# Weights of the experts fetched into the merged stream's memory, token tile by token tile

## The chip, the cores and the metric

The kernel runs on one core of a Trainium2 chip. The metric is device time in microseconds of one execution, as the median of the runs shown. A profile is taken of one more execution of the same program. TensorE is PE in the rows, VectorE DVE, ScalarE ACT, GpSimd POOL, SyncE SP.

## The reference, cut to what matters

Two transformer blocks for 512 tokens of width 1024, in float32. The change lies in the second block: the end of its token mixer and its mixture of experts.

```python
def token_mixer(...):                       # attention and state-space branch, then
    merged = g_attn * (attn @ nsa_w_o) + g_ssm * (ssm @ ssm_w_o)      # 512 x 1024
    return merged @ w_out                                            # 1024 x 1024

def hier_moe(h, ...):
    g_prob = softmax(xt @ w_group + b_group); g_p, g_idx = top_k(g_prob, 1)   # 4 groups
    e_logits = (xt @ w_expert + b_expert)[its group's 8]
    e_p, e_idx = top_k(softmax(e_logits), 2)                                 # 2 of 8
    w = g_p * e_p / sum(e_p)
    # each expert e on the rows routed to it, added up with weights w:
    (silu(xb @ w_gate[e]) * (xb @ w_up[e])) @ w_down[e]      # 32 experts, width 256
...
x = x + gate1 * token_mixer(norm1(x)); x = x + gate2 * hier_moe(norm2(x)); out = rmsnorm(x, final_g)
```

The last line is in short form: both norms are modulated by a vector c, and a final norm ends the program.

## The kernel before

The program is emitted by Python functions. A scheduler sets each engine's order of instructions from the order of emission and its own estimates of when operands are ready; every DMA that SyncE issues stands in SyncE's one row and waits there for its buffer.

**merge** (L1856) forms the merged stream in columns of 128 features by 512 tokens, transposed (features on partitions), and splits each into a rounded half `m_hi` (ACT, L1885) and a rest `m_lo` (VectorE, L1886), so that w_out's product is three products of halves. `m_hi` and `m_lo` hold all 512 tokens, 16 KB on each partition.

**Moe.mix_out** (L1940) is w_out's product with the residual. The first half of the output columns comes from `K.ts` (L252 to L254), over 4 groups of weights, in each over the 4 token tiles. The second half runs over token tiles t = 0 to 3 (L2057 to L2059), 24 products for each. After a tile, `residual` adds it to x (`xres` in the rows) and stores the new x into DRAM (`xa`, L1965). `logits0` and `logits1(t)` make the router's logits `lg` and the normed row h (L2014 on VectorE for the last tile), stored into DRAM as `hd` (L2039).

**Moe.route** (L2065) picks groups and experts on VectorE, ranks the tokens of each expert, and by products with one-hot matrices (`slots`, L2164: first `hb`, then `val`, then `vf`) makes the lists `idx`, `dst` and `wsl`. A gather on GpSimd (L2268) fetches the rows of `hd` for a pair of experts, two experts of 64 rows each. `spread` (L2308) transposes them. Its small tiles lie in the pool "eh".

**Moe.run** (L2366) goes through 17 entries: 16 pairs and, at position 12, one overflow entry whose expert number is read from `ove`. For each entry: `up` (L2322, 32 products: 8 slices k, gate and up, two experts), tanh and two products on ACT and VectorE, `down` (L2344), scatter into `yd`. Then the final norm reads `xa` and `yd`.

**The ring.** `load` (L2270) fetches the weights of an entry in units of 1 MB, one DMA at L2280 each: gate, up, down for both experts of a pair, 99 units in all. `raw` (L1931) gives the buffers in turn: 18 before, of 11 buffers of its own (pool "er"), 5 of pool "er2" in the memory of `m_hi` and `m_lo`, opened once these are closed, and the two halves of x. `fetch(n)` emits loads until n units are asked for: 11 in mix_out ahead of w_out's second half, 13 and 16 in `open` (the last three behind `self.stored`, the last store of hd), and 18 in `route`:

```python
hold = nc.sync.dma_start(K.dram.tile([128, 1], F32, name="hold"), self.xg[0][:, 0:1]).ins
with tc.issue_after(hold):
    self.fetch(sum(NR) + 2)
```

The hold (L2173) stores 4 bytes of each of the 128 rows of the first gathered tile into a DRAM tile that nobody reads. It waits for the gather, and the two units behind it wait for its issue.

Of the kernel before, what the change touches and what calls it, by code (L numbers as in the profile page):

```python
# [9 lines left out]
F32 = mybir.dt.float32  # L10
F32R = mybir.dt.float32r
# [7 lines left out]
T = 512  # L19
# [51 lines left out]
class Filler:  # L71


    def __init__(self):
        self.q = []
# [1777 lines left out]
                yield from K.ws_pieces(K.i["ssm_w_o_2"][0], c * 128, 256, shi, slo, 4, branch)  # L1853


def merge(K, st, gd, aT, m_hi, m_lo):  # L1856

    nc, tc, i = K.nc, K.tc, K.i
    P = lambda *a, **k: st.enter_context(K.pool(*a, **k))
    mp = P(name="mm_", bufs=1)  # L1860
    wp = P(name="mw", bufs=2)
    a_hi, a_lo = (mp.tile([128, 4, T], F32R, name=n) for n in ("a_hi", "a_lo"))
    for c in range(4):
        nc.scalar.copy(a_hi[:, c, :], aT[0][:, c, :])
        nc.vector.tensor_sub(a_lo[:, c, :], aT[0][:, c, :], a_hi[:, c, :].bitcast(F32))
    x = [(h[:, c, :], l[:, c, :]) for h, l in ((a_hi, a_lo), aT[1:]) for c in range(4)]
    for c in range(0, 8, 2):
        sg = {}
        for b in range(2):
            for e in range(2):  # L1870
                sg[b, e] = wp.tile([128, T], F32, name=f"sg{b}{e}")
                nc.sync.dma_start(sg[b, e], gd[b, c + e])
        aps = [K.mm() for _ in range(2)]
        for u in (4, 0):
            hi, lo = K.wload(i["nsa_w_o_2"][0][u * 128:(u + 4) * 128, c * 128:c * 128 + 256], 4, 256)
            for e in range(2):
                for k in range(4):
                    (xh, xl), s = x[u + k], slice(e * 128, e * 128 + 128)
                    nc.tensor.matmul(aps[e], hi[:, k, s], xh, start=u + k == 4, stop=False)
                    nc.tensor.matmul(aps[e], hi[:, k, s], xl, start=False, stop=False)  # L1880
                    nc.tensor.matmul(aps[e], lo[:, k, s], xh, start=False, stop=u + k == 3)
        for e, p in enumerate(aps):
            nc.vector.scalar_tensor_tensor(sg[0, e], sg[0, e], 1.0, p, op0=OP.add, op1=OP.mult)
            nc.gpsimd.tensor_add(sg[0, e], sg[0, e], sg[1, e])
            nc.scalar.activation(m_hi[:, c + e, :], sg[0, e], AF.Copy, scale=0.5)  # L1885
            nc.vector.scalar_tensor_tensor(m_lo[:, c + e, :], sg[0, e], 0.5, m_hi[:, c + e, :].bitcast(F32),  # L1886
                                           op0=OP.mult, op1=OP.subtract)


NE = 32  # L1890
# [1 line left out]
FAR = 128  # L1892
NPAIR = NE // 2
NOV = 15
NR = 11, 5
NX = 3
AHEAD = 2
FAR_AT = 12
# [6 lines left out]
class Moe:  # L1905
# [3 lines left out]
    def __init__(self, K, st):  # L1909

        nc, i = K.nc, K.i
        self.K, self.sc = K, []
        P = lambda *a, **k: st.enter_context(K.pool(*a, **k))
        cp = self.cp = P(name="ec", bufs=1, side="right")
        self.x = cp.tile([128, NT, D], F32, name="xres2")
        self.ss = cp.tile([128, 2, NT], F32, name="ss2")
        self.er = [P(name="er", bufs=NR[0], side="right")]
        self.nraw = 0
        flat = lambda a, k: a.rearrange("e (p k) n -> e p (k n)", k=k)
        self.wd = [flat(i[n][0], k) for n, k in (("moe_w_gate_2", 8), ("moe_w_up_2", 8), ("moe_w_down_2", 2))]  # L1920

        self.order = [8 * a + e for e in range(8) for a in range(2)]
        self.order.insert(FAR_AT, None)
        self.ready, self.loads = [], self.weights()
        self.cst = cp.tile([128, ECOLS], F32, name="ecst")
        nc.sync.dma_start(self.cst, i["ce"])
        self.xa = K.dram.tile([T, D], F32, name="xa")

        self.yd = K.dram.tile([2 * T, D], F32, name="yd")

    def raw(self):  # L1931

        k = self.nraw % (sum(NR) + 2)
        self.nraw += 1
        if k >= sum(NR):
            k -= sum(NR)
            return self.x[:, 2 * k:2 * k + 2, :].rearrange("p t n -> p (t n)")
        pool = next(p for j, p in enumerate(self.er) if k < sum(NR[:j + 1]))
        return pool.tile([128, 2048], F32, name="eraw")

    def mix_out(self, xd, mod, m_hi, m_lo):

        K, cp, x, ss = self.K, self.cp, self.x, self.ss
        nc, i = K.nc, K.i
        w = i["w_out_2"][0]
        for t in range(NT):
            nc.sync.dma_start(x[:, t, :], xd[t * 128:(t + 1) * 128, :])
        self.hd = K.dram.tile([T, D], F32, name="hd")
        self.lg = cp.tile([128, NT, 36], F32, name="lg")
        with K.pool(name="mo", bufs=2) as wp:  # L1950
# [56 lines left out]
            def logits1(t):  # L2007
# [28 lines left out]
                else:  # L2036
                    nc.scalar.activation(h, h, AF.Copy, scale=rs)
                    nc.gpsimd.tensor_add(h, h, sh2)
                self.stored = nc.sync.dma_start(self.hd[t * 128:(t + 1) * 128, :], h).ins  # L2039

            wt = []
            for u in range(4):
# [1 line left out]
                r3 = raw.rearrange("p (k n) -> p k n", k=2)  # L2044
                nc.sync.dma_start(r3, w[u * 256:(u + 1) * 256, 512:].rearrange("(k p) n -> p k n", p=128))
                wt.append(K.split(raw, pool=None if u < 3 else wp, bufs=3 if u < 3 else 1))
            self.fetch(NR[0])
            for t in range(NT):
                if t == 1:
                    logits0()  # L2050
                if t > 1:
                    logits1(t - 2)
                ps = K.mm()
                for k in range(8):
                    hi, lo = (a[:, (k % 2) * 512:(k % 2 + 1) * 512] for a in wt[k // 2])
                    tt = slice(t * 128, (t + 1) * 128)
                    nc.tensor.matmul(ps, m_hi[:, k, tt], hi, start=k == 0, stop=False)  # L2057
                    nc.tensor.matmul(ps, m_hi[:, k, tt], lo, start=False, stop=False)
                    nc.tensor.matmul(ps, m_lo[:, k, tt], hi, start=False, stop=k == 7)  # L2059
                residual(1, t, ps)  # L2060
            for t in (2, 3):
                logits1(t)

    def route(self):
# [15 lines left out]
        with K.pool(name="eh", bufs=2, side="right") as hp, ExitStack() as late:  # L2080
# [89 lines left out]
            q1 = places(rk, iota, "roh")  # L2170
            at = index(idx[:, :NPAIR], slots(q1, hb)[:, :NPAIR], T).ins
            self.gather(self.xg[0], idx[:, 0:1])
            hold = nc.sync.dma_start(K.dram.tile([128, 1], F32, name="hold"), self.xg[0][:, 0:1]).ins  # L2173
            with tc.issue_after(hold):
                self.fetch(sum(NR) + 2)
            late.enter_context(tc.issue_after(at))

            def softmax(src, m, n, nm):
# [134 lines left out]
    def up(self, xt, rw):  # L2313
# [2 lines left out]
        nc = K.nc  # L2316
        pg, pu = ph = [K.mm()[:, :256] for _ in range(2)]
        sl = EH if len(rw) == 2 else (slice(0, FAR),)
        for k in range(8):
            for n in range(2):  # L2320
                for s, r in zip(sl, rw):
                    nc.tensor.matmul(ph[n][s], xt[:, k, s], r[n][:, k * 256:(k + 1) * 256],  # L2322
                                     start=k == 0, stop=k == 7)
# [32 lines left out]
    def open(self, st, mod):  # L2356
# [1 line left out]
        self.g2 = bcast(K, st.enter_context(K.pool(name="ef", bufs=1)), mod["g2"], "g2row")  # L2358
        self.wp = st.enter_context(K.pool(name="ew", bufs=2))
        self.xg = [K.wraw() for _ in range(NX)]  # L2360

        self.fetch(NR[0] + 2)
        with K.tc.issue_after(self.stored):
            self.fetch(sum(NR))

    def run(self, st, out):  # L2366
        K = self.K
# [128 lines left out]
def block2(K, x, B, mats, mod, out):  # L2496
# [20 lines left out]
            nc.vector.tensor_sub(slo[:, c, :], sT[:, c, :], shi[:, c, :].bitcast(F32))  # L2517
        N.attend(aT, shi, slo, gd)
    mp = mst.enter_context(K.pool(name="mrg", bufs=1))
    m_hi = mp.tile([128, 8, T], F32R, name="m_hi")  # L2520
    m_lo = mp.tile([128, 8, T], F32R, name="m_lo")
    with ExitStack() as st:
        merge(K, st, gd, aT, m_hi, m_lo)
    alst.close()
    B.st.close()
    K.close_x()
    with ExitStack() as st:
        moe = Moe(K, st)
        moe.mix_out(xd, mod, m_hi, m_lo)
        mst.close()  # L2530
        moe.er.append(st.enter_context(K.pool(name="er2", bufs=NR[1])))
        moe.open(st, mod)
        moe.route()
        moe.run(st, out)


def body(tc, i, out):
# [66 lines left out]
```

## Time and profile before

| | us |
|---|---|
| runs | 1674.64, 1672.14, 1673.77; median 1673.77 |
| profiled execution, its own time | 1672.8 |
| its span, first to last instruction | 1671.0 |
| PE busy | 1564.5 (94%) |
| DVE busy | 933.6 (56%) |
| ACT busy | 635.6 (38%) |
| POOL busy | 235.7 (14%) |
| mean granted clock of PE | 0.981 |

The device time has 1.8 us around the span. Busy time is an average over stages with different limits; the page's slices of the span show the DMA engines at a tenth to seven tenths for most of it and at nine tenths or more in the last fifth, where the experts' weights are read.

### The profile page before, as it was taken

The numbers are of one execution on the slowest core, as the hardware profiler recorded it, in microseconds if no ns is written. First come the engines' busy times: TensorE is split into PE (matmuls) and PEld (weight loads), VectorE is DVE, ScalarE is ACT, GpSimd is POOL, SyncE is SP. The second block draws the span as 40 slices with busy tenths as digits, with TensorE's granted clock in tenths as the row PEclk, the third lists the DMA queues.
The fourth block names the chain that finished last, engine by engine and source line by source line (L and its number), as shares of the span: only waits on it lengthen the run. The fifth ranks groups of instructions, "written<-read, shape, count | busy, mean of one in ns | idle before, by whom it ended". The sixth has DMA issues, their size and how long they took to land. (4 is left out here: it accounts for less than half of the span.)

```text
span 1671.0 us, 25319 instructions
## 1 busy us (share of the span) xinstructions
PE 1564.5 (94%) x9568; PEld 1171.6 (70%) x9568; DVE 933.6 (56%) x2155; ACT 635.6 (38%) x1300; POOL 235.7 (14%) x270
## 2 busy tenths in 40 slices
PE   6999999999999999999999899999999988999981
PEld 5677777778777888788788667676678755554550
DVE  6764368558989866556576545555534463221114
ACT  4543346554422332345343555555643320010001
POOL 1212211100010000004220111121212221110102
PEclk9999999999999999999999999999999998999996
DMA  4221121137467967325863322111127869999994
GB/s 147 69 77 52 52 102 64 64 88 211 148 216 205 210 214 216 103 89 165 177 154 113 89 64 64 51 40 56 45 75 265 302 256 326 418 418 418 419 397 178
DMA packets 204305, 284.74 MB, mean 170 GB/s; under 512 B 75666, under 2 KB 150421, under 8 KB 191509
## 3 DMA queue, kind: packets, MB, share of 16 engines
q1 hardware_dynamic: 198370, 273.07, 49.6%
q0 software_dynamic: 4896, 8.40, 1.3%
q10 hardware_dynamic: 915, 1.64, 0.3%
q8 instruction: 76, 1.25, 0.3%
q14 instruction: 48, 0.39, 0.1%
HBM read 262.07 MB, written 30.43 MB: 175 GB/s over the span
## 5 line engine op out<-in xcount | busy, mean ns | idle before, releaser
L154 DVE TENSOR_TENSOR wlo<-wraw,whi 128x1024 fp32r<-128x1024 f32 x162 | 203.4, 1257 | 155.0 <-ACT whi L153 153.3
L153 ACT CAST whi<-wraw 128x1024 fp32r<-128x1024 f32 x164 | 171.6, 1049 | 243.3 <-PE mm L1055 71.9
L213 PE MATMUL mm<-hhi,whi 128*128 128x512 f32 x440 | 184.2, 419 | 5.4 <-DVE mx L1757 2.9
L215 PE MATMUL mm<-hhi,wlo 128*128 128x512 f32 x440 | 176.6, 402 | 0.1
L214 PE MATMUL mm<-hlo,whi 128*128 128x512 f32 x440 | 176.3, 401 | 0.0
L2322 PE MATMUL mm<-eraw,xt 128*64 128x256 f32 (+1 forms) x1024 | 126.8, 382 | 7.2 <-DMA eraw<-in_moe_w_up 3.6
L171 PE MATMUL mm<-hhi,whi 128*128 128x512 f32 x320 | 127.4, 398 | 0.2 <-ACT whi L153 0.2
L172 PE MATMUL mm<-hlo,whi 128*128 128x512 f32 x320 | 126.3, 395 | 0.0
L173 PE MATMUL mm<-hhi,wlo 128*128 128x512 f32 x320 | 125.9, 395 | 0.0
L2322 PEld LDWEIGHTS mm<-eraw,xt 128*64 128x64 f32 (+1 forms) x1024 | 84.2, 139 | 46.4 <-DMA eraw<-in_moe_w_up 5.6
L213 PEld LDWEIGHTS mm<-hhi,whi 128*128 128x128 f32 x440 | 83.0, 189 | 32.7 <-issue 8.3
L215 PEld LDWEIGHTS mm<-hhi,wlo 128*128 128x128 f32 x440 | 83.1, 189 | 20.5 <-issue 1.6
L214 PEld LDWEIGHTS mm<-hlo,whi 128*128 128x128 f32 x440 | 83.2, 189 | 18.7 <-issue 4.7
L1760 ACT ACTIVATE NP<-NP,mx 128x512 f32<-128x512 f32 (+3 forms) x128 | 72.1, 563 | 44.3 <-DVE mx L1757 43.6
L1757 DVE CUSTOM_DVE_ANT_0 NP<-mm,ncst 128x512 f32<-128x512 f32 (+3 forms) x128 | 61.4, 479 | 37.6 <-PE aux L1788 35.9
L171 PEld LDWEIGHTS mm<-hhi,whi 128*128 128x128 f32 x320 | 60.2, 188 | 15.4 <-issue 0.8
L1054 PE MATMUL mm<-wlo,ahi 128*128 128x512 f32 x176 | 69.3, 394 | 1.5 <-DVE wlo L154 1.5
L2348 DVE SCALAR_TENSOR_TENSOR ey<-mm,wsl,g2row 128x512 f32<-128x512 f32 x34 | 25.5, 750 | 80.4 <-PE mm L2344 80.4
L173 PEld LDWEIGHTS mm<-hhi,wlo 128*128 128x128 f32 x320 | 60.3, 188 | 14.3
L1053 PE MATMUL mm<-whi,ahi 128*128 128x512 f32 x176 | 69.9, 401 | 0.0
L172 PEld LDWEIGHTS mm<-hlo,whi 128*128 128x128 f32 x320 | 60.3, 188 | 13.6
L1055 PE MATMUL mm<-whi,alo 128*128 128x512 f32 x176 | 69.3, 394 | 0.0
(786 smaller groups left out, 3279.0 us busy)
## 6 DMA issues: line engine op xcount, KB each, us to landing
wraw<-in_w_in SPq DMA_DIRECT2D x68, 512.0 KB
eraw<-in_moe_w_gate SPq DMA_DIRECT2D x32, 1024.0 KB
eraw<-in_moe_w_up SPq DMA_DIRECT2D x32, 1024.0 KB
eraw<-in_moe_w_down SPq DMA_DIRECT2D x25, 1024.0 KB
araw<-in_ada_w SPq DMA_DIRECT2D x48, 512.0 KB
wraw<-in_w_gate SPq DMA_DIRECT2D x22, 512.0 KB
wraw<-in_w_up SPq DMA_DIRECT2D x22, 512.0 KB
wraw<-in_w_down SPq DMA_DIRECT2D x22, 512.0 KB
```

The lines of the kernel that those rows point to most:

```text
L153: nc.scalar.copy(hi[:, :m], raw[:, :m])
L154: (eng or nc.vector).tensor_sub(lo[:, :m], raw[:, :m], hi[:, :m].bitcast(F32))
L171: nc.tensor.matmul(o, hi[:, k, a:a + m], xhi[:, kk, :], start=kk == 0, stop=False)
L172: nc.tensor.matmul(o, hi[:, k, a:a + m], xlo[:, kk, :], start=False, stop=False)
L173: nc.tensor.matmul(o, lo[:, k, a:a + m], xhi[:, kk, :], start=False, stop=kk == nk - 1)
L213: nc.tensor.matmul(ps, hi, xhi[:, k, :], start=k == 0, stop=False)
L214: nc.tensor.matmul(ps, hi, xlo[:, k, :], start=False, stop=False)
L215: nc.tensor.matmul(ps, lo, xhi[:, k, :], start=False, stop=k == nk - 1)
L1053: nc.tensor.matmul(ps, a[:, tt], hi[:, k, :], start=kk == 0, stop=False)
L1054: nc.tensor.matmul(ps, a[:, tt], lo[:, k, :], start=False, stop=False)
L1760: nc.scalar.activation(p[:, :n], p[:, :n], AF.Exp, scale=-1.0, bias=m, accum_out=d)
L2322: nc.tensor.matmul(ph[n][s], xt[:, k, s], r[n][:, k * 256:(k + 1) * 256], start=k == 0, stop=k == 7)
```

## The change

The merged stream becomes four tiles `m`, one for each token tile, with both halves in each (128 x 2 x 8 x 128); `merge` writes each column in four pieces on ACT and on VectorE. A tile is free when the second half of w_out's product for its token tile is through, and the ring takes it then. The ring has 19 buffers: 11 of its own, tiles 0, 1, 2 of m, the first half of x, tile 3, one of pool "er2", the second half of x, and one of pool "er3", opened on the right side after `route` in memory of its pool "eh". `fetch` goes by tile: to 12, 13, 14 units behind tiles 0, 1, 2, to 15 ahead of tile 3, to 16 behind it, to 18 in `open`; the 19th is asked for in `run`. The hold is gone. In `up` the loop over gate and up stands outside the loop over k, so that all 16 gate products come ahead of the 16 up products.

```diff
-                nc.scalar.activation(m_hi[:, c + e, :], sg[0, e], AF.Copy, scale=0.5)
-            nc.vector.scalar_tensor_tensor(m_lo[:, c + e, :], sg[0, e], 0.5, m_hi[:, c + e, :].bitcast(F32),
-                                           op0=OP.mult, op1=OP.subtract)
+            for t in range(NT):
+                v = sg[0, e][:, t * 128:(t + 1) * 128]
+                hi, lo = (m[t][:, h, c + e, :] for h in range(2))
+                nc.scalar.activation(hi, v, AF.Copy, scale=0.5)
+                nc.vector.scalar_tensor_tensor(lo, v, 0.5, hi.bitcast(F32), op0=OP.mult, op1=OP.subtract)
...
     def raw(self):
-        k = self.nraw % (sum(NR) + 2)
+        k = self.nraw % (NER + 8)
         self.nraw += 1
-        if k >= sum(NR):
-            k -= sum(NR)
+        if k < NER:
+            return self.er[0].tile([128, 2048], F32, name="eraw")
+        k -= NER
+        if k in (3, 6):
+            k = k // 3 - 1
             return self.x[:, 2 * k:2 * k + 2, :].rearrange("p t n -> p (t n)")
-        pool = next(p for j, p in enumerate(self.er) if k < sum(NR[:j + 1]))
-        return pool.tile([128, 2048], F32, name="eraw")
+        if k in (5, 7):
+            return self.er[k // 2 - 1].tile([128, 2048], F32, name="eraw")
+        return self.mp.tile([128, 2048], F32, name="eraw", tag="m", bufs=NT)
...
-            self.fetch(NR[0])
+            self.fetch(NER)
             for t in range(NT):
                 if t == 1:
                     logits0()
                 if t > 1:
                     logits1(t - 2)
+                if t == 3:
+                    self.fetch(NER + 4)
...
                 residual(1, t, ps)
+                self.fetch(NER + (1, 2, 3, 5)[t])
...
             self.gather(self.xg[0], idx[:, 0:1])
-            hold = nc.sync.dma_start(K.dram.tile([128, 1], F32, name="hold"), self.xg[0][:, 0:1]).ins
-            with tc.issue_after(hold):
-                self.fetch(sum(NR) + 2)
...
-        for k in range(8):
-            for n in range(2):
+        for n in range(2):
+            for k in range(8):
                 for s, r in zip(sl, rw):
                     nc.tensor.matmul(ph[n][s], xt[:, k, s], r[n][:, k * 256:(k + 1) * 256],
                                      start=k == 0, stop=k == 7)
...
-        self.fetch(NR[0] + 2)
-        with K.tc.issue_after(self.stored):
-            self.fetch(sum(NR))
+        self.fetch(NER + 7)
...
-        mst.close()
-        moe.er.append(st.enter_context(K.pool(name="er2", bufs=NR[1])))
+        moe.er.append(st.enter_context(K.pool(name="er2", bufs=1)))
         moe.open(st, mod)
         moe.route()
+        moe.er.append(st.enter_context(K.pool(name="er3", bufs=1, side="right")))
         moe.run(st, out)
+    mst.close()
```

SyncE's row, before, from the first store of xa to the second turn of the ring (`xa` and `hd` are stores, `eraw<-in_moe...` units of weights, `xres_12812<-in_moe...` units into halves of x):

```order
267 L1965 DMA xa<-xres_12812 128x1024 x2
268 L2039 DMA hd<-wraw 128x1024
269 L1965 DMA xa<-xres_12812 128x1024
270 L2039 DMA hd<-wraw 128x1024
271 L1965 DMA xa<-xres_12812 128x1024
272 L2039 DMA hd<-wraw 128x1024
273 L2280 DMA eraw<-in_moe_w_down 128x2048
274 L2039 DMA hd<-wraw 128x1024
275 L2280 DMA eraw<-in_moe_w_gate 128x2048 x2
276 L2280 DMA eraw<-in_moe_w_up 128x2048 x2
277 L2173 DMA hold<-wraw 128x1
278 L2280 DMA xres_12812<-in_moe_w_down 128x2048 x2
279 L2280 DMA eraw<-in_moe_w_gate 128x2048 x2
```

SyncE's row after, the same place (the code's lines are moved by 20: L1985 is xa, L2059 hd, L2300 the units):

```order
267 L1985 DMA xa<-xres_12862 128x1024
268 L2300 DMA eraw<-in_moe_w_down 128x2048
269 L1985 DMA xa<-xres_12862 128x1024
270 L2300 DMA eraw<-in_moe_w_gate 128x2048
271 L2059 DMA hd<-wraw 128x1024
272 L1985 DMA xa<-xres_12862 128x1024
273 L2300 DMA eraw<-in_moe_w_gate 128x2048
274 L2059 DMA hd<-wraw 128x1024
275 L2300 DMA xres_12862<-in_moe_w_up 128x2048
276 L1985 DMA xa<-xres_12862 128x1024
277 L2300 DMA eraw<-in_moe_w_up 128x2048
278 L2059 DMA hd<-wraw 128x1024 x2
279 L2300 DMA eraw<-in_moe_w_down 128x2048
280 L2300 DMA xres_12862<-in_moe_w_down 128x2048
281 L2308 TENSOR_LOAD ove
```

Units 12 to 16 stand between the stores of the token tiles, the last two directly behind the last hd, and the hold and the wait behind it are gone; a load of `ove` stands ahead of the 19th unit.

VectorE's row, before, at the last logits of mix_out, the last steps of the reciprocal root and the first step of routing (`tgm`):

```order
1774 L262 TENSOR_SCALAR rsi<-msv 128x1
1775 L2014 TENSOR_TENSOR wraw<-xres_12812,G 128x1024
1776 L264 TENSOR_SCALAR rsy<-rsi 128x1
1777 L267 TENSOR_TENSOR rsa<-rsy 128x1
1778 L268 SCALAR_TENSOR_TENSOR rsb<-rsa,msv 128x1
```

```order
1783 L272 SCALAR_TENSOR_TENSOR rsy<-rsb,rsy 128x1
1784 L2021 SCALAR_TENSOR_TENSOR l_13004<-l_13004,rsy,rb 128x36
1785 L2026 SCALAR_TENSOR_TENSOR lg<-aux,rsy,l_13004 128x36
1786 L2094 TENSOR_REDUCE tgm<-lg 128x4
1787 L2095 TENSOR_TENSOR tge<-lg,tgm 128x16
```

VectorE's row after, the same place (L2034 is h = x G, L2046 the logits, L2117 routing's first step):

```order
1782 L272 SCALAR_TENSOR_TENSOR rsy<-rsb,rsy 128x1
1783 L2041 SCALAR_TENSOR_TENSOR l_13054<-l_13054,rsy,rb 128x36
1784 L2046 SCALAR_TENSOR_TENSOR lg<-aux,rsy,l_13054 128x36
1785 L2034 TENSOR_TENSOR wraw<-xres_12862,G 128x1024
1786 L2117 TENSOR_REDUCE tgm<-lg 128x4
1787 L2118 TENSOR_TENSOR tge<-lg,tgm 128x16
1788 L2121 SCALAR_TENSOR_TENSOR tge<-tge,ecst 128x16
```

The product of 128 x 1024 moved from between two steps of the root to a place ahead of routing's first step.

## Rows read from the trace of the kernel before

**Rows 1.** Stretches of the span: busy time by engine, granted clock, DMA share and rate.
```profile
core 0: us, PE busy (x) PEld busy (x) DVE busy (x) ACT busy (x) POOL busy (x), PEclk, DMA share, GB/s
...
1352.00:1356.00 4.00, 4.00 (x25) 3.38 (x24) 3.21 (x3) 1.55 (x4) 3.04 (x2) 1.00 0.00 0
1356.00:1360.00 4.00, 3.56 (x18) 2.70 (x16) 3.56 (x13) 0.37 (x2) 1.74 (x1) 1.00 0.66 262
...
1360.00:1376.00 16.00, 11.45 (x43) 6.61 (x43) 12.02 (x47) 4.39 (x10) 0.68 (x3) 0.92 0.64 214
1376.00:1386.00 10.00, 5.00 (x23) 4.79 (x23) 6.26 (x47) 0.34 (x2) 3.31 (x3) 0.50 1.01 416
...
1388.00:1390.00 2.00, 2.00 (x10) 1.40 (x11) 0.69 (x2) 0.59 (x1) 0.00 (x0) 0.50 1.80 64
1390.00:1392.00 2.00, 2.00 (x16) 1.32 (x12) 0.67 (x3) 0.00 (x0) 0.00 (x0) 0.91 0.27 37
...
1397.00:1398.00 1.00, 1.00 (x12) 0.67 (x10) 0.00 (x0) 0.00 (x0) 0.29 (x1) 1.00 0.82 336
...
1520.00:1600.00 80.00, 74.04 (x431) 43.20 (x428) 15.22 (x26) 6.71 (x15) 8.05 (x8) 1.00 1.02 419
...
core 0: us, PE busy (x), PEclk, DMA share, GB/s
...
1417.76:1430.40 12.64, 12.14 (x92) 1.00 1.02 417
```

**Rows 2.** Timeline of PE, end of routing, pairs 0 and 3 (products record double).
```profile
start us, us, engine line op out<-in xcount [idle before <-releaser]
...
1382.32 3.59 PE L2164 MATMUL aux<-val,roh 128*128 128x32 f32 x16 [4.91 <-DVE val L2205]
1387.30 1.97 PE L2308 MATMUL aux<-ident,wraw 128*128 128x128 f32 x8 [1.39 <-DMA wraw<-hd,idx]
...
1393.10 6.26 PE L2322 MATMUL mm<-eraw,xt 128*64 128x256 f32 x54
...
1430.41 7.08 PE L2322 MATMUL mm<-eraw,xt 128*64 128x256 f32 x64
```

**Rows 3.** Timeline of SyncE, from w_out's second half to pair 0.
```profile
1355.29 0.32 SPq L1965 DMA_DIRECT2D xa<-xres  x1
...
1387.27 0.33 SPq L2173 DMA_DIRECT2D hold<-wraw  x1
1387.69 0.85 SPq L2280 DMA_DIRECT2D xres<-in_moe_w_down  x2
1398.55 0.82 SPq L2280 DMA_DIRECT2D eraw<-in_moe_w_gate  x2
```

**Rows 4.** DMA view of 1388 to 1397 us: packets; queue, packets, MB, share.
```profile
DMA packets 209, 0.37 MB, mean 41 GB/s; under 512 B 159, under 2 KB 159, under 8 KB 168
...
q1 hardware_dynamic: 185, 0.34, 67.1%
```

**Rows 5.** Timeline of POOL, the first and the fourth gather.
```profile
1378.50 1.23 POOL L2268 DMA_INDIRECT wraw<-hd,idx  x1 [10.56 <-DVE sgd L2183]
...
1396.31 0.99 POOL L2268 DMA_INDIRECT wraw<-hd,idx  x1 [13.89 <-DMA hold<-wraw]
```

**Rows 6.** Waits of PE from 1490 to 1640 us.
```profile
engine line waited for: us in total, times, longest us
...
PE mm L2322 <- DMA eraw<-in_moe_w_up: 3.6, 3, 1.4
```

**Rows 7.** Timeline of PE, products of pair 8 and of the last pair.
```profile
1497.47 4.10 PE L2322 MATMUL mm<-eraw,xt 128*64 128x256 f32 x34
1502.66 3.67 PE L2322 MATMUL mm<-eraw,xt 128*64 128x256 f32 x30 [1.09 <-DMA eraw<-in_moe_w_up]
...
1621.29 3.67 PE L2322 MATMUL mm<-eraw,xt 128*64 128x256 f32 x32 [1.65 <-DMA eraw<-in_moe_w_gate]
1626.78 3.67 PE L2322 MATMUL mm<-eraw,xt 128*64 128x256 f32 x30 [1.82 <-SPq L2394]
```

**Rows 8.** Timeline of DVE, logits of the last token tile.
```profile
1362.55 1.23 DVE L2014 TENSOR_TENSOR wraw<-xres,G 128x1024 f32<-128x1024 f32 x1
...
1367.17 0.26 DVE L2026 SCALAR_TENSOR_TENSOR lg<-aux,rsy,l 128x36 f32<-128x36 f32 x1 [1.68 <-PE aux L2024]
```

**Rows 9.** Timelines of DVE and of PE, end of the merge.
```profile
1305.74 0.69 DVE L1886 SCALAR_TENSOR_TENSOR m_lo<-sg,m_hi 128x512 fp32r<-128x512 f32 x1 [1.85 <-ACT m_hi L1885]
...
1301.24 0.40 PE L252 MATMUL mm<-whi,m_hi 128*128 128x512 f32 x1
```

More of the change, by code (lines that the diff above doesn't have):

```diff
@@ L1853, in merge_side, with __init__, __getitem__, merge @@
                 yield from K.ws_pieces(K.i["ssm_w_o_2"][0], c * 128, 256, shi, slo, 4, branch)
-def merge(K, st, gd, aT, m_hi, m_lo):
+class ByToken:
+    def __init__(self, m, h):
+        self.m, self.h = m, h
+    def __getitem__(self, at):
+        _, k, s = at
+        return self.m[s.start // 128][:, self.h, k, :]
+def merge(K, st, gd, aT, m):
     nc, tc, i = K.nc, K.tc, K.i
@@ L1894 @@
 NOV = 15
-NR = 11, 5
+NER = 11
 NX = 3
@@ L1916, in __init__ @@
         self.ss = cp.tile([128, 2, NT], F32, name="ss2")
-        self.er = [P(name="er", bufs=NR[0], side="right")]
+        self.er = [P(name="er", bufs=NER, side="right")]
         self.nraw = 0
@@ L1931, in raw, with mix_out @@
     def raw(self):
-        k = self.nraw % (sum(NR) + 2)
+        k = self.nraw % (NER + 8)
         self.nraw += 1
-        if k >= sum(NR):
-            k -= sum(NR)
+        if k < NER:
[3 more added lines that the diff above has]
+            k = k // 3 - 1
             return self.x[:, 2 * k:2 * k + 2, :].rearrange("p t n -> p (t n)")
-        pool = next(p for j, p in enumerate(self.er) if k < sum(NR[:j + 1]))
-        return pool.tile([128, 2048], F32, name="eraw")
-    def mix_out(self, xd, mod, m_hi, m_lo):
+        if k in (5, 7):
+            return self.er[k // 2 - 1].tile([128, 2048], F32, name="eraw")
+        return self.mp.tile([128, 2048], F32, name="eraw", tag="m", bufs=NT)
+    def mix_out(self, xd, mod, mp, m):
         K, cp, x, ss = self.K, self.cp, self.x, self.ss
@@ L1945, in mix_out @@
         w = i["w_out_2"][0]
+        self.mp = mp
+        m_hi, m_lo = ByToken(m, 0), ByToken(m, 1)
         for t in range(NT):
@@ L2038, in logits1 @@
                     nc.gpsimd.tensor_add(h, h, sh2)
-                self.stored = nc.sync.dma_start(self.hd[t * 128:(t + 1) * 128, :], h).ins
+                nc.sync.dma_start(self.hd[t * 128:(t + 1) * 128, :], h)
             wt = []
@@ L2519, in block2 @@
     mp = mst.enter_context(K.pool(name="mrg", bufs=1))
-    m_hi = mp.tile([128, 8, T], F32R, name="m_hi")
-    m_lo = mp.tile([128, 8, T], F32R, name="m_lo")
+    m = [mp.tile([128, 2, 8, 128], F32R, name="m", tag="m", bufs=NT) for _ in range(NT)]
     with ExitStack() as st:
-        merge(K, st, gd, aT, m_hi, m_lo)
+        merge(K, st, gd, aT, m)
     alst.close()
@@ L2528, in block2 @@
         moe = Moe(K, st)
-        moe.mix_out(xd, mod, m_hi, m_lo)
-        mst.close()
-        moe.er.append(st.enter_context(K.pool(name="er2", bufs=NR[1])))
+        moe.mix_out(xd, mod, mp, m)
+        moe.er.append(st.enter_context(K.pool(name="er2", bufs=1)))
         moe.open(st, mod)
         moe.route()
+        moe.er.append(st.enter_context(K.pool(name="er3", bufs=1, side="right")))
         moe.run(st, out)
+    mst.close()
 def body(tc, i, out):
```

## The prediction

> **What bounds the kernel now.** I read the page first: TensorE is busy 94% of the span, but its DMA line stands near 9 for the last sixth only, where the experts run. So I asked for rates in stretches [rows 1]. Among the experts the DMA engines are full: 417 GB/s at a share of 1.02 in 1418 to 1430, 419 at 1.02 in 1520 to 1600. What they carry is 99 units of weights of 1 MB (1.049 million bytes): 2.51 us each at 418 GB/s, about 2.8 us with the gathers and scatters that share the engines. Six units make a pair of experts, so the stream gives a pair in 15 to 17 us. TensorE starts faster, with 12.64 us for a pair [rows 1], and eats the ring empty; from 1490 us on it waits for up weights (3.6 us in all [rows 6]), and in the last pair for gates (1.65) and once more for 1.82 us [rows 7]. That last wait is put down to SyncE's sequencer, but it stands between gate and up products, where only the up weights can be missing. TensorE's start and its end thus hang on the stream: **what brings the stream forward brings the last up products (1626.78) forward**, and the 44 us behind them (products, scatter, final norm, end at 1671.0) follow unchanged.
>
> Then the stretch ahead of it. At 1376 to 1386 the engines move 416 GB/s; from 1388 on 64 GB/s at a share of 1.80, then 37 at 0.27, and at 1397 336 again [rows 1]. The DMA view of these 9 us has 209 packets, 159 of them under 512 bytes; SyncE's queue moves 0.34 MB, and its packets take 67.1% of the engines' time [rows 4]. Elsewhere a share of 1.02 buys 419 GB/s; here two thirds of one buy 38. What starts at 1387.27 is the hold, 128 pieces of 4 bytes into DRAM, and right behind it the two units for the halves of x [rows 3]. GpSimd's fourth gather waits 13.89 us for the hold to land and starts at 1396.31 [rows 5], one step before the rate comes back. I take it that the hold's small writes clog the engines and that units 17 and 18 crawl behind them.
>
> **The change, part by part.**
>
> *No hold, units 12 to 18 early.* At 1397 units 17 and 18 have moved 0.34 of 2.10 MB; the other 1.76 MB take 4.2 us at 418 GB/s. So unit 18 is in at **1401.2** and unit 19 at 1401.2 + 2.51 = **1403.7** (0.3 more with a gather beside it). After, SyncE issues units 12 to 16 between the stores of w_out's token tiles and 17 and 18 behind the last hd, ahead of routing. There the engines have room: 0, 262 and 214 GB/s in 1352 to 1376, and 416 in the next 10 us for units that now go earlier [rows 1]. Seven units are 17.6 us; I put them in by 1382.
>
> *The 19th buffer* lies in memory of routing and is free when routing's last slot products (vf) are through, which is when the products of pair 0 go on, 1393.10 [rows 2]. From issue to data I take 1.4 us. The rows give bounds: behind the store of xa issued at 1355.29 [rows 3] the engines move nothing until 1356, and 4.00 us at 262 GB/s, 1.05 MB, by 1360 [rows 1], which is 2.5 us of full rate, so the lag was 0.7 to 2.2. Unit 19 is in at 1393.0 + 1.4 + 2.5 = **1397.0**. Gain: 1403.7 - 1397.0 = 6.7 us (5.9 to 7.4; up to 0.3 more for the gather).
>
> *Gates ahead of ups.* Before, gate and up products alternate, and pair 0's gate buffers are refilled from 1398.55 on [rows 3]. Behind the vf slots stand 54 records, 27 of the 32 products, 6.26 us, 0.232 us each [rows 2]. With the 16 gate products first, 11 stand behind 1393.1: the buffers are free at 1393.1 + 11 x 0.232 = 1395.6, and units 20 and 21 start by 1397.0, as unit 19 ends: a bubble of 0 to 0.5 us, I take 0.3. Issued at 1398.55 they would leave a bubble of 2.9, so some 2.6 of the 6.7 us hang on this edit. Later requests follow TensorE's products at 12.64 us a pair, faster than the stream takes them. In the late pairs the edit also closes up a row: before, single products stand alone among pairs (34 records 4.10 us, 30 records 3.67 [rows 7], against 7.08 for 64 [rows 2]). That gives TensorE 0.7 us back in each of some eight pairs, where it then waits longer for weights: 0 at the end.
>
> *Routing.* VectorE's h = x G of the last token tile (1.23 us) moves from inside the chain of the reciprocal root to behind the last logits at 1367.17, ahead of the top-1 chain [rows 8]: about 1.1 us on the chain to the val slots, which end at 1382.32 + 3.59 + 1.1 = 1387.0 [rows 2]. Before, TensorE then waited 1.39 us for the first gather, which stood behind units 13 to 16, and spread at 1387.30 [rows 2]. With those units mostly in, the gather should land near 1384, and the spread starts at 1387.0: -0.3 us. Bounds: -2 (the granted clock is .50 here [rows 1]; without that gap it may rise sooner) and +2 (the gather lands late).
>
> *Merge by token tile.* A write of 128x512 becomes four of 128x128, on ACT and on VectorE. VectorE's takes 0.69 us, the last one ending at 1306.4 [rows 9]; four pieces cost between nothing and 3 x 0.69 = 2.1 us more for each of the last two, so the last ends by 1311 at worst. Its columns are wanted by the last of four groups of 24 products, 72 x 0.232 = 16.7 us behind 1301.24 [rows 9], 1317.9. Cost 0; without that cover 4 us.
>
> *The loads of ove on SyncE, moved forward,* wait for a value written near 1382, and nothing behind them can go before 1393: 0, and perhaps -0.1 at the tail.
>
> **Sum.** -6.7 (stream) + 0.3 (bubble) - 0.1 = -6.5 us. TensorE itself can give that much: 0.3 at the start, 7.1 us of waits [rows 6, 7], and the pairing. The profiled execution took 1672.8 us: 1666.3. The median of the runs stands 1.0 us above it: **1667.3**, -0.39%. What a measurement of this kernel can tell from no change is about 0.2%, 3.3 us.
>
> **The rivals.**
>
> *The crawl is not the hold's.* Then it comes back with the first unit that starts into idle engines behind a gather: unit 19 from 1394.4 moves a third of itself in 9 us and is in near 1404, against 1403.7: **1673 to 1674**, no change. For it: in the later part of the crawl the share is 0.27 [rows 1], no picture of clogged engines. Against it: a gather issued at 1378 to 1381 does no harm to 416 GB/s [rows 1], and the rate returns just as the hold lands [rows 1, 5]. Chance 0.12. The Trainium skill, page "DMA: Bandwidth & Descriptors", section Anatomy of one DMA, gives a transfer (of GpSimd's path) a fixed cost of 2.0 us; by that estimate the hold is through near 1389.3, 7 of the 9 us are something else's, and the time is this rival's. The same page's Specifications say that below 512 bytes an engine reads, modifies and writes, which the hold's 4 bytes would meet. The trace bears out a dear hold: GpSimd, waiting for it alone, goes on 9 us behind its issue [rows 5].
>
> *The ring does not feed it.* If the refill of unit 19 or of the gates comes later than I work out (another last reader of that memory, another order of issue), only the hold's part is left, about half: **1670.5**, on the border. Against it: TensorE's pace is ahead of the stream from the first pair. Chance 0.12.
>
> *Clock.* Without the gap before the spread the clock (0.50 until 1388 to 1390, 0.91 in 1390 to 1392 [rows 1]) rises up to 2 us sooner; vf slots, unit 19 and the gates come 1 to 2 us sooner: **1665.5**. Chance 0.12.
>
> *Slower: the gather unprotected.* The hold kept two units out of the way of the first gather. If units 16 to 18 are still queued when it is issued (1379.6), it lands 3 x 2.5 us later, at 1388.5, 1.5 us late: **1668.5**, still faster; chance 0.08. From a landing after 1393.5 on, 6.5 us late, it eats the gain. That takes five or more units ahead of it, as there were before (the hold, waiting for the gather, stood until 1387.27), and stores of hd late besides: SyncE works in order, and hd of the last tiles stands behind x's first half, which waits for the store of xa and a square on ACT. **1676**, chance 0.04.
>
> **How the numbers follow.** My forecast has 0.52. Faster by over 0.2% gets 0.78 (forecast, clock, mild gather, half of the ring), within 0.2% 0.17 (the crawl and most of the rest of the ring), slower 0.05. The likeliest has 1665.8 to 1668.8 for itself (lag, bubble, spread of the runs). The range of 8 in 10 reaches from 1664.0 (clock) to 1671.5: it takes in mild gather and ring and leaves out crawl and bad gather.
>
> **What the profile after would show.** Right: no stretch under 100 GB/s from 1395 to the end of the stream; the gates' refill issued near 1395.6 instead of 1398.55; val slots 1 us later, and no wait of TensorE for the gather; the last up products near 1620.3. Wrong: low GB/s with a share far from 1 behind 1394 (crawl); TensorE waiting for the first gather; a DMA share under 0.95 between 1410 and 1590, or no waits for weights in the last pairs, so that TensorE's own work sets the end.

## The result, and the profile after

| | before | after |
|---|---|---|
| median of 4 runs each, us | 1672.95 (1670.25 to 1674.64) | 1662.26 (1661.67 to 1663.11) |
| ratio, 95% interval | | 0.994 [0.9924, 0.9956] |
| span of the profiled execution | 1671.0 | 1660.3 |
| PE, DVE, ACT, POOL busy | 1564.5, 933.6, 635.6, 235.7 | 1561.1, 937.2, 637.6, 235.5 |
| mean granted clock | 0.981 | 0.983 |

Faster by 0.6%, 7 to 13 us. The direction and most of the steps came as predicted; the time is 5.0 us under the predicted 1667.3 and 1.7 under the lower end of its range, 1664.0. Two of the timed runs below, one of e1 (7201 us) and one of e13 (4740 us), were in a slow state and are in no ratio.

The two spans differ by 10.7 us. Before reading any of it as the change's, I looked for an event ahead of the change that both traces have: the issue of the first store of xa on SyncE. SyncE after (start, us, engine, line, operation, tiles, count):

```profile
1330.74 0.33 SPq L1985 DMA_DIRECT2D xa<-xres  x1
1331.16 0.38 SPq L2300 DMA_DIRECT2D eraw<-in_moe_w_down  x1
...
1372.37 1.19 SPq L2300 DMA_DIRECT2D xres<-in_moe_w_down  x1
1389.01 2.65 SPq L2300 DMA_DIRECT2D eraw<-in_moe_w_gate  x2
1391.75 3.37 SPq L2300 DMA_DIRECT2D eraw<-in_moe_w_up  x2
```

Before, that store is issued at 1334.06: 3.3 of the 10.7 us lie ahead of it. Over all seven profiles of kernels with the front of before it stands between 1328.93 and 1335.47, and over ten with the changed front between 1329.93 and 1335.53: much the same spread, so one profile of each says nothing of the stretch ahead. **From here on times are counted from this store ("from xa").** To the end of the span that is 336.94 us before and 329.56 after: 7.4 less. With the repetitions below, before has 336.9, 337.8, 337.4 (mean 337.4), after 329.6, 330.3, 329.0, 329.4 (mean 329.6): **7.8 us less**.

Where they come from, PE's stretches after (stretch, length, PE busy and records, granted clock, DMA share, GB/s):

```profile
1380.00:1384.00 4.00, 4.00 (x20) 0.50 0.74 249
1384.00:1388.00 4.00, 4.00 (x23) 0.69 0.16 41
1388.00:1390.00 2.00, 2.00 (x19) 1.00 0.00 0
1390.00:1392.00 2.00, 2.00 (x22) 1.00 0.99 262
1392.00:1394.00 2.00, 2.00 (x22) 1.00 1.07 418
1394.00:1396.00 2.00, 2.00 (x18) 1.00 0.92 369
1396.00:1398.00 2.00, 1.94 (x15) 1.00 1.03 430
1398.00:1400.00 2.00, 2.00 (x12) 1.00 1.01 426
```

A unit is 128 packets of 8192 bytes on SyncE's queue (q1), so units can also be counted in the traces by these packets. The last packet of unit 18 goes out at 1381.37; from there to 1389.9 the queue of the weights moves nothing, and only GpSimd's queue of gathers is at work (DMA view of 1381.72 to 1389.9 us):

```profile
q0 software_dynamic: 466, 0.62, 25.5%
```

In place of nine crawling microseconds [rows 1, 4] all 18 units are in by 1381.7, and unit 19 starts in 1390 to 1392: 262 GB/s for 2 us are 0.524 MB, 1.25 us of 418 GB/s, so by this estimate at 1390.75, **60.0 from xa**. Before, by the prediction's estimate, unit 18 ended at 1401.2, 67.1 from xa; by the packets its last one went out at 1401.75. TensorE's row and GpSimd's fourth gather after:

```profile
1379.28 3.59 PE L2187 MATMUL aux<-val,roh 128*128 128x32 f32 x16 [4.89 <-DVE qi L2261]
1382.81 1.97 PE L2328 MATMUL aux<-ident,wraw 128*128 128x128 f32 x8
...
1388.91 6.26 PE L2342 MATMUL mm<-eraw,xt 128*64 128x256 f32 x54
...
1616.22 3.67 PE L2342 MATMUL mm<-eraw,xt 128*64 128x256 f32 x30 [1.81 <-DMA eraw<-in_moe_w_up]
```

```profile
1385.05 0.99 POOL L2288 DMA_INDIRECT wraw<-hd,idx  x1 [3.18 <-PE aux L2328]
```

Against [rows 2] the wait of 1.39 us ahead of the spread is gone, and against [rows 5] the fourth gather waits 3.18 us for a product in place of 13.89 for the hold. The last up products start at 1616.22, 285.5 from xa, where they stood at 292.7 [rows 7], and still wait for their weights. The waits of PE from 1470 to 1640 (waited for: us in all, times, longest):

```profile
PE mm L2342 <- DMA eraw<-in_moe_w_up: 4.4, 3, 1.8
PE mm L2342 <- DMA eraw<-in_moe_w_gate: 1.7, 1, 1.7
```

So the stream still sets the end; it only starts sooner.

### The profile page after: what moved, and what is told of

It is laid out like the page before. It is cut to its first block, busy times and chain, and to the rows that moved or that the text cites. A ratio compares the mean times of both kernels' runs of the same rounds, so it can differ in the third digit from the quotient of the medians.

```text
span 1660.3 us, 25364 instructions
## 1 busy us (share of the span) xinstructions
PE 1561.1 (94%) x9568; PEld 1164.8 (70%) x9568; DVE 937.2 (56%) x2179; ACT 637.6 (38%) x1324; POOL 235.5 (14%) x270
## 3 DMA queue, kind: packets, MB, share of 16 engines
q8 instruction: 76, 1.25, 0.3%
## 5 line engine op out<-in xcount | busy, mean ns | idle before, releaser
L2342 PEld LDWEIGHTS mm<-eraw,xt 128*64 128x64 f32 (+1 forms) x960 | 79.7, 139 | 46.6 <-DMA eraw<-in_moe_w_up 5.7
L171 PEld LDWEIGHTS mm<-hhi,whi 128*128 128x128 f32 x320 | 60.2, 188 | 15.4 <-issue 0.8
L2364 PE MATMUL mm<-eraw,ea 128*64 128x512 f32 x232 | 69.2, 601 | 1.8 <-ACT ea L2358 1.0
L173 PEld LDWEIGHTS mm<-hhi,wlo 128*128 128x128 f32 x320 | 60.2, 188 | 14.3
L172 PEld LDWEIGHTS mm<-hlo,whi 128*128 128x128 f32 x320 | 60.3, 188 | 13.6
```

What stands on the lines that cost most here:

```text
L171: nc.tensor.matmul(o, hi[:, k, a:a + m], xhi[:, kk, :], start=kk == 0, stop=False)
L172: nc.tensor.matmul(o, hi[:, k, a:a + m], xlo[:, kk, :], start=False, stop=False)
L173: nc.tensor.matmul(o, lo[:, k, a:a + m], xhi[:, kk, :], start=False, stop=kk == nk - 1)
```

## The experiments

The theory: what counts is the stream's restart, from which it runs on without a hole (unit 19's first data, estimated from the rates as above; where a hole follows that unit, its length is added), and the end follows it one for one. Two rivals: the hold's crawl by itself is the cost; or the order of gate and up products is, by itself.

**The hold, at before.** Three kernels: before unchanged; the hold with whole 512-byte pieces; no hold.

> The kernel before, unchanged, as a yardstick. Between the two profiled executions 3.3 us of the 10.7 us lie ahead of 1232 us, in code that the change doesn't touch. Theory A (these 3.3 us are not of the change but spread between executions): the ratio is 1.000 with an interval of some +-0.001 to 0.002, and in this profile the store of xa of the first token tile (1334.06 before, 1330.74 after) stands 1 us or more off 1334.06. Rival (the 3.3 us are a lasting effect of the change): the copy stands at 1334.06 within 0.5 us.

```diff
# e2
-K.dram.tile([128, 1], F32, name="hold"), self.xg[0][:, 0:1]
+K.dram.tile([128, 128], F32, name="hold"), self.xg[0][:, 0:128]
# e3
-hold = nc.sync.dma_start(...).ins
-with tc.issue_after(hold):
-    self.fetch(sum(NR) + 2)
+self.fetch(sum(NR) + 2)
```

> Before, with the hold storing 128 pieces of 512 bytes instead of 128 of 4; same place, same waits. Theory A (the small pieces clog the engines): the stretch of 9 us under 100 GB/s is gone, units 17 and 18 are in 5 us behind the hold (near 1394 instead of 1401), the fourth gather starts 2 to 3 us behind the hold instead of 9. The stream then stands still until the gates are refilled (1398.5), so unit 19 comes only 1.2 us sooner: -1 us, 0 to -2.5. Rival B (the crawl is not the hold's): the stretch stays as it is, 0 us.

> Before, without the hold; units 17 and 18 are asked for without waiting for it, and SyncE's row has the first of them ahead of the store of hd of tile 2. Theory A: no crawl; the stream stands still until the gates are refilled (1398.5 or later), so -1 us if the first gather is not late. Rival C (the hold protected the first gather): with seven units in front of it the gather lands 2 to 5 us later, the first products with it, and the time is +1 to +4 us. Rival B: crawl stays, about 0.

Measured: 0.9992 [0.998, 1.0004], 1.0001 [0.9988, 1.0015], 0.999 [0.9979, 1.0002]. None is faster by more than the runs can tell; the intervals of e2 and e3 leave room for a gain of at most 2.0 and 3.5 us. Yet e2's crawl is gone. Its SyncE, its GpSimd, and PE's stretches:

```profile
1386.37 0.33 SPq L2173 DMA_DIRECT2D hold<-wraw  x1
...
1398.81 0.80 SPq L2280 DMA_DIRECT2D eraw<-in_moe_w_gate  x2
```

```profile
1389.32 1.03 POOL L2268 DMA_INDIRECT wraw<-hd,idx  x1 [7.54 <-DMA hold<-wraw]
```

```profile
1390.00:1392.00 2.00, 2.00 (x9) 0.52 0.93 393
1392.00:1394.00 2.00, 2.00 (x19) 1.00 0.95 391
1394.00:1396.00 2.00, 2.00 (x22) 1.00 0.10 33
1396.00:1398.00 2.00, 2.00 (x22) 1.00 0.00 0
...
1400.00:1402.00 2.00, 1.66 (x15) 1.00 0.70 270
```

The two units that took the engines from 1388 to 1401.8 before are through by about 1395, and the hold has landed 2.95 us behind its issue, in place of 9. Then the engines stand empty until gates are asked for at 1398.81: the ring is full, and no buffer comes free before TensorE has read one. The crawl is the hold's, and taking it away alone is worth nothing that the runs show. The first rival falls.

e3, without a hold, has no crawl either, but there the first gather stands behind more units. TensorE's spread waits for it, and the gates are asked for at 1402.07 only, 66.6 from xa:

```profile
1389.85 1.97 PE L2306 MATMUL aux<-ident,wraw 128*128 128x128 f32 x8 [2.45 <-DMA wraw<-hd,idx]
```

Its end is 338.0 from xa, about as before.

**The gates, at before.** `for n` outside `for k` in `up`, with a second repetition of before and of after on the same chip.

> Before, with nothing changed but the loop in up: gate products ahead of up products; the hold stays. Theory A (the stream sets the end): units 17 and 18 crawl until about 1401 whatever the gates do, so the refill of the gates 3 us sooner only makes a queue: 0 us (-0.7 to +0.3), and time from the store of xa to the end as before's, 336.9 to 337.8. Rival F (the edits add up, each worth its 2.3 us): -2.3 us, 335.

> Before, unchanged, on the same chip as the next two. The first store of xa came at 1333.2 to 1335.5 in the four profiles of before's kind and at 1329.9 to 1332.6 in the six of after's kind. Theory A (spread between executions and chips): here the two kinds overlap, within 1.5 us. Rival (a lasting effect of the change on code that it doesn't touch): this one and the one before it at 1333 to 1335.5, the next two at 1330 to 1332.5.

> After, unchanged, on the same chip. Time from the store of xa to the end 329.5 to 330.5 by either theory; theory A -7.5 us against before in the runs (ratio 0.9955), the rival -10 (0.994).

Measured: 0.9996 [0.9983, 1.0009], 1.0006 [0.999, 1.0021], 0.9944 [0.9926, 0.9962]. In e9 the gates are asked for at 1390.21 already, 61.3 from xa, but units 17 and 18 crawl and are in at about 1396.8 only, and the stream restarts at 67.9, as in e10 (67.7). The second rival falls too. Alone neither edit gives anything that the runs show: the crawl and the full ring are two waits in a row, and each edit takes only one of them away.

**Both, at before.** e2 and e9 together.

> Before with both edits that did nothing each by itself: the hold in pieces of 512 bytes (ratio 1.000) and gate products first (0.9996). Theory A (the stream's restart needs both, units 17 and 18 out of the crawl and a buffer free): units 17 and 18 are in 5 to 8 us behind the hold, the gates are refilled some 4 us sooner than with the wide hold alone, and the stream starts 3 to 4.5 us sooner; time from the store of xa to the end 333 to 334.5 instead of 337.4. Rival F (the edits add up): 337, no change.

Measured: 0.9975 [0.9965, 0.9985], 4.6 us between the medians (1666.48 against 1671.11). The gain is there in the timed runs. Its profiled execution does not show it: 337.9 from xa, as before, where 333 to 334.5 was expected. PE's stretches:

```profile
1390.00:1392.00 2.00, 2.00 (x12) 0.50 0.53 203
1392.00:1394.00 2.00, 2.00 (x10) 0.50 0.00 0
1394.00:1396.00 2.00, 2.00 (x12) 0.50 0.00 0
1396.00:1398.00 2.00, 2.00 (x18) 0.86 0.32 57
1398.00:1400.00 2.00, 2.00 (x21) 1.00 0.90 356
```

In that execution the granted clock stays at 0.50 (the level of 1.2 GHz) until 1396.56, 66.2 from xa; before it came back at 56.3, in e2 at 58.7. Pair 0's gate products run at the lower clock, the refill is issued at 1396.43, and the stream restarts at 67.9. The profiled execution took the longest of the ten that count, with the lowest mean clock (1670.1 us at 0.978; the other nine 1664.29 to 1669.58 at 0.980 to 0.984). That fits timed runs with the clock back sooner, but as only one execution was profiled it is argued, not shown.

**The parts of the change, taken out of after.** After unchanged (e5); with the hold of 4-byte pieces put back behind the first gather, without a wait of the units on it (e4); without the 19th buffer (e6: `% (NER + 7)`, no pool "er3"); with gate and up alternating (e7: `for k` outside `for n`); e6 and e7 together (e8).

```diff
# e4
 self.gather(self.xg[0], idx[:, 0:1])
+nc.sync.dma_start(K.dram.tile([128, 1], F32, name="hold"), self.xg[0][:, 0:1])
```

> After, with the hold put back (128 pieces of 4 bytes of the first gathered tile, waited for by the fourth gather); no unit waits for it in the program, but it stands in SyncE's row ahead of unit 19. Theory A: a crawl of some 8 us from the landing of the first gather on; this is over near 1391, so unit 19, asked for at 1389, loses 0 to 2 us: +0 to +2 us on after, and the fourth gather starts 8 us behind the hold. Rival B (the crawl comes with units that start into idle engines): no crawl here, and 0 us, gather 4 within 2.5 us of the hold.

> The kernel after, unchanged, for its time beside the others. In code ahead of 1330 us the five profiles so far spread by 4.7 us at the same place (store of xa of the first token tile: 1330.74 to 1335.47), so what counts is the time from there to the end: 336.9 and 337.8 us for the two profiles of before, 329.6 for the one of after. Theory A: the ratio is 0.9955 (-7.5 us), and the profile again gives 329 to 330.5 us from xa to the end. Rival (all 10.7 us are of the change): ratio 0.9935.

> After, with a ring of 18 (no buffer in the memory of routing's pool). Unit 19 then waits for the first gate buffer. Theory A (the stream, which stands still until the ring gives a buffer, sets the end): gates are free 11 products of 0.232 us behind the vf slots, 2.5 us later than the 19th buffer, so the end is 2.5 us later than after's, 1.5 to 3.2; the stretch without transfers ahead of the stream is as much longer. Rival E (earlier units and the missing hold are what counts, the last buffer doesn't): 0 us.

> After, with gate and up products alternating as before (loop over k outside). Unit 19 goes out as in after; the gate buffers come free at the end of all 32 products. Theory A: a hole of about 3 us in the stream behind unit 19, and the end 2.5 to 3.5 us later than after's. Rival D (TensorE's own row, in which single products stand alone in eight late pairs, 0.7 us each): 5 us or more later, with no waits for weights left in the late pairs. Rival E: 0 us.

> After, with a ring of 18 and alternating products: only the missing hold, the early units 12 to 18 and the split merge are left of the change. Theory A: the stream stands still from about 1380 until the gates are refilled at the end of the first pair's products, as in the runs of before with a wide hold or none (ratios 1.000 and 0.999); 5.5 to 6.5 us later than after, -1 to -2.5 us against before (ratio 0.9985 to 0.9995). Rival E (early units are the gain): still -5 us or more.

| | ratio to before [95%] | restart from xa | end from xa | end - restart |
|---|---|---|---|---|
| e5 after | 0.9947 [0.9934, 0.996] | 60.2 | 330.3 | 270.1 |
| e4 hold put back | 0.9962 [0.995, 0.9974] | 60.7 | 330.7 | 270.0 |
| e6 no 19th buffer | 0.9949 [0.9936, 0.9962] | 62.9 | 331.9 | 269.0 |
| e7 gate and up mixed | 0.9958 [0.9945, 0.9972] | 62.9 | 332.2 | 269.3 |
| e8 both off | 0.9964 [0.9951, 0.9977] | 65.3 | 333.5 | 268.2 |
| e10 before | 1.0006 [0.999, 1.0021] | 67.7 | 337.4 | 269.7 |

The timed ratios lie too close together to part e5 to e8. The traces do it, one for each kernel: the restart moves over 7.5 us, and what lies behind it stays at 268.2 to 270.1, as the theory has it. The packets say the same without an estimate: in the fifteen profiles with a ring of 18 or 19 buffers the last packet of unit 20 is in between 65.0 and 74.9 us from xa, and the end comes 262.9 to 265.0 later. A third rival, that TensorE's earlier start by itself is the gain, falls with the traces too: in e5 to e8 the spread starts at 52.0 to 52.7 from xa alike, and the ends lie 3.1 us apart. Against the mean of after (329.6, with 1.3 us between its four profiles), the 19th buffer is worth 2.3 us, the order of gates 2.6, both 3.9, where 5.5 to 6.5 were expected; and what is left in e8 (early units, no hold) is worth 3.9 against before, where its expectation had one to two and a half. It is more than e2 and e3 gave, in part because TensorE frees the gates sooner: they are asked for at 63.6 from xa in e8, at 65.6 in e2 and 66.6 in e3, and the clock comes back at 55.8 against 58.7 and 59.5. These 2.0 and 3.0 us are the larger part of the 3.8 and 4.5 by which e8 ends ahead of the two; the rest stays open. How the mixed order costs its share, PE's stretches of e7 and of e8:

```profile
1390.00:1392.00 2.00, 2.00 (x22) 1.00 0.83 283
1392.00:1394.00 2.00, 2.00 (x22) 1.00 0.54 225
1394.00:1396.00 2.00, 2.00 (x18) 1.00 0.31 49
1396.00:1398.00 2.00, 1.93 (x13) 1.00 0.97 389
```

```profile
1392.00:1394.00 2.00, 2.00 (x20) 1.00 0.00 0
1394.00:1396.00 2.00, 2.00 (x15) 1.00 0.59 172
1396.00:1398.00 2.00, 1.94 (x11) 1.00 0.99 418
```

In e7 unit 19 starts as early as in e5 and then nothing is there to follow it; in e8 nothing moves before 1394.

In e4 no unit of weights stands right behind the hold. SyncE, GpSimd, and the DMA view of 1383 to 1391 us:

```profile
1382.88 0.33 SPq L2196 DMA_DIRECT2D hold<-wraw  x1
```

```profile
1391.20 0.99 POOL L2289 DMA_INDIRECT wraw<-hd,idx  x1 [9.60 <-DMA hold<-wraw]
```

```profile
DMA packets 262, 0.19 MB, mean 24 GB/s; under 512 B 219, under 2 KB 219, under 8 KB 261
...
q1 hardware_dynamic: 144, 0.00, 1.0%
```

It still takes 8.3 us from issue to landing, at 1.0% of the engines' time on its queue: all 144 packets of that queue have gone out by 1384.5, and what the landing waits for in the 6.7 us that follow the trace does not show. But this falls into the time when the engines have little else to do, and by the trace it costs 1.1 us.

**A 20th buffer.** If the theory holds, a buffer more should fill the pause of 1382 to 1390 in the stream of weights. Memory for it: the third tile of "whi" and the third of "wraw", half a unit each, at the price of one gathered pair less in advance.

```diff
-NX = 3
-AHEAD = 2
+NX = 2
+AHEAD = 1
-        k = self.nraw % (NER + 8)
+        k = self.nraw % (NER + 9)
+        if k == 7:
+            return self.spare
...
+        self.spare = Halves(K.w.tile([128, 1024], F32, name="spa", tag="whi", bufs=3), K.wraw())
-        self.fetch(NER + 7)
+        self.fetch(NER + 8)
```

> After, with a 20th buffer that is free before routing ends: the third tile of the transposed rows and the third gather buffer, which are free once w_out is done (rows are gathered one pair ahead instead of two). Its unit falls into the time from about 1383 to 1390 in which after moves nothing. Theory A: one unit more is in when the stream begins, so the end is 2.5 us earlier than after's, 2.0 to 3.0, if the shorter lead of the gathers costs nothing. Rival: the stream is not what sets the end by now (TensorE, with 6 us of waits for weights left, is): 0 us.

Measured: 0.9961 [0.9949, 0.9974], end 330.3 from xa: no gain. The first gather now has another unit ahead of it, which the prediction had as a rival for the change itself. PE:

```profile
1387.86 1.97 PE L2347 MATMUL aux<-ident,wraw 128*128 128x128 f32 x8 [2.49 <-DMA wraw<-hd,idx]
1389.62 3.48 PE L2201 MATMUL aux<-vf,rof 128*128 128x45 f32 x16
1393.03 8.51 PE L2361 MATMUL mm<-eraw,xt 128*64 128x256 f32 x64
```

The spread waits 2.49 us for it, the clock comes back at 1395.86 only (62.6 from xa, against 55.7 in after), and the first gate buffer is filled again (with up weights) only by the load of 1398.11, 64.8 from xa against 60.6 in after. So the next kernel asks for that unit behind a hold of 512-byte pieces on the first gather; e2 had shown such a hold to be cheap.

```diff
 self.gather(self.xg[0], idx[:, 0:1])
+hold = nc.sync.dma_start(K.dram.tile([128, 128], F32, name="hold"), self.xg[0][:, 0:128]).ins
+with tc.issue_after(hold):
+    self.fetch(NER + 8)
```

> After with the 20th buffer, its unit now asked for behind the landing of the first gather (a hold in pieces of 512 bytes stands in SyncE's row ahead of it). Theory A: the gather lands as in after, TensorE's row is after's, the unit moves in 1384 to 1388 when nothing else does, and the end is 2.5 us earlier than after's: 327 us from the store of xa to the end, 326.3 to 328. Rival (TensorE or the loss of gathers' lead is the bound now): 329.5 or more.

> After, unchanged, beside the run before this one on the same chip: 329 to 330.3 us from the store of xa to the end by theory A, whatever the store's own time is (1329 to 1334).

Measured: e14 0.9938 [0.9924, 0.9951], 1660.42 us; after beside it 0.9954 [0.994, 0.9967], 1663.85. From xa 327.27 against 329.35. SyncE of e14 has the extra unit, in two halves, right behind the hold:

```profile
1387.48 0.33 SPq L2210 DMA_DIRECT2D hold<-wraw  x1
1387.86 0.42 SPq L2319 DMA_DIRECT2D spa<-in_moe_w_gate  x1
1388.34 0.42 SPq L2319 DMA_DIRECT2D wraw<-in_moe_w_gate  x1
```

Its one trace is 2.1 us shorter than that of after beside it, in the range expected by the theory (326.3 to 328); the intervals of the timed runs overlap, so that it beats after is not shown by time alone.

## Why the prediction was right in direction and too slow

- **The crawl is the hold's: right** (e2, e4). The rival that something else makes it is out: with 512-byte pieces the two units behind the hold move at 391 to 393 GB/s. The 512-byte pieces landed in 2.95 us (e2), the 4-byte pieces in 8.3 us with no weights behind them (e4). The Trainium skill, page "DMA: Bandwidth & Descriptors", section Anatomy of one DMA, has a fixed cost of 2.0 us for GpSimd's path, while the hold is issued by SyncE; the first is not far from it, the second is four times as long. Its Specifications, by which an engine reads, modifies and writes below 512 bytes, agree with the second being dear, but no run here shows that mechanism. Nor does the trace show small writes that keep the engines busy, as "clog" has it: in e4 the queue of the hold takes 1.0% of their time.
- **Unit 19 after: right, put a little too late.** Predicted 1394.4 for its start, 60.3 from xa; by the rates 60.0 to 60.2 in the unchanged repetitions, with the first packets out at 59.0 to 59.6. It is asked for at 58.3 in the profile after, where the prediction had 58.9.
- **Gates ahead of ups: 2.6 predicted, 2.6 measured** (e7). That the two agree so closely is in part luck, with 1.3 us between the profiles of after. The bubble, taken as 0.3, is about 0.1: 1390.75 to 1400 moved 3.81 MB, which at 418 GB/s is 9.1 of 9.25 us.
- **"Only the hold's part is left, about half": right in number, not in its cause.** e8, without the ring's gains, has 3.9 of 7.8 us left. But the hold's part by itself is nothing that the runs show (e2, e3); in e8 it counts, for the larger part because the gates are also asked for 2.0 and 3.0 us sooner than there.
- **Routing: the 1.1 us came, and did not matter.** VectorE after:

```profile
1363.85 0.26 DVE L2046 SCALAR_TENSOR_TENSOR lg<-aux,rsy,l 128x36 f32<-128x36 f32 x1 [2.71 <-PE aux L2044]
1364.02 1.28 DVE L2034 TENSOR_TENSOR wraw<-xres,G 128x1024 f32<-128x1024 f32 x1
1365.22 0.16 DVE L2117 TENSOR_REDUCE tgm<-lg 128x4 f32<-128x16 f32 x1
```

The chain starts 1.37 us behind the logits, yet the val slots start at 48.5 from xa against 48.3: the granted clock stood at 1.00 in 1370 to 1376, so that the products of `hb`, at 1373.2 to 1374.1, took 0.26 us each, where before, at 1375.5 to 1377.0, they took 0.36. The gather is in time, and the spread starts at 52.1 from xa against 53.2: -1.2 in place of -0.3. In two of the four profiles of after (e5, e15) the clock did not help so: the val slots start at 49.2 to 49.3, and the gain at the spread is 0.4 to 0.5 us against the mean of before (53.1). The rival "Clock" came in part: over the four the clock is back at 55.4 to 55.9, against 56.2 to 56.6 in the three of before.
- **Merge by token tile: 0, right.** VectorE's last write after is four pieces in 0.90 us, at 1302, in place of one in 0.69, and TensorE waits for none of them.

```profile
1302.22 0.90 DVE L1900 SCALAR_TENSOR_TENSOR m<-sg,m 128x128 fp32r<-128x128 f32 x4 [1.53 <-ACT m L1899]
```

- **The sum, "-6.7 (stream) + 0.3 (bubble) - 0.1 = -6.5 us": this step failed, in the stream's term.** The prediction had unit 19 in at 1403.7 before and at 1397.0 after, 69.6 and 62.9 from xa, and bounds of 5.9 to 7.4 us around the 6.7 (0.3 more for a gather). By the packets the last one of unit 19 goes out at 70.3 before and 62.5 after: 7.8 us. The larger part is before's: "the other 1.76 MB take 4.2 us at 418 GB/s" took 4.76 us, 370 GB/s, with a gather beside them on another queue (DMA view of before, 1397 to 1401.76 us):

```profile
q1 hardware_dynamic: 237, 1.76, 89.2%
q0 software_dynamic: 70, 0.11, 5.9%
```

The rest is unit 19 after, asked for 0.7 us sooner than predicted. From xa to the end the change gives 7.4 us between these two traces and 7.8 between the means of three and four.
- **"The range of 8 in 10 reaches from 1664.0 (clock) to 1671.5": this failed too.** All four medians of after (1661.36 to 1663.85) lie under the range's lower end, so one lucky measurement is not the reason. Of the 5.0 us by which the forecast was missed, the base is one part: it was counted from 1673.8, the median of three runs, and the medians of before taken later lie between 1671.1 and 1672.95. The stretch ahead of the change is another: of the spans, predicted 1671.0 - 6.5 = 1664.5 and measured 1660.3, 0.9 us are the sum and 3.3 lie ahead of the first store of xa. They are there already near 975 us, ahead of the merge, in code that the change does not touch. I had three runs of before within 2.5 us and took that for the spread; the seven profiles with its front differ by 6.5 us at that store alone.

What stays open: the timed ratios of the four repetitions of after (0.994 to 0.9954) have a mean of 0.9946, 9.0 us, the traces give 7.8 from xa. Whether a microsecond of it is a lasting effect ahead of xa (the stores and reads of `m`) or chance can't be told: the mean issue of that store is 1332.7 with the front of before and 1331.9 with that of after, each spread over 5.6 us or more.

## What to carry to other kernels

In a stream that is full from some point on, find the moment from which it has no hole any more, and count the change by how far that moment moves; edits that each take away one of two waits in a row can show nothing alone and a gain together (4.6 us in the timed runs of e13). A DMA used only as an order mark was cheaper here with 512-byte pieces: as 4-byte pieces it took 8.3 to 9.0 us and held back what was queued behind it. Before two profiles are compared, align them at an event ahead of the change, and put the spread at that event into the range.

## What the runs showed of the hardware that was not expected

A store of 128 pieces of 4 bytes into DRAM took 8.3 us from issue to landing with no weights moving (e4) and 9.0 us with two units behind it (before), one of 128 pieces of 512 bytes 2.95 us (e2), and only the first held up the units behind it. The granted clock of the same stretch came back at 55.7 us from xa (after), 56.3 (before), 58.7 (e2), 59.5 (e3) and 66.2 (e13), and the profile in which it came latest shows none of the gain that the timed runs of the same kernel have.
